# A one-core transformer layer: two one-tile pieces at the opening, an identity made on the chip, and a last addition in two halves

## The chip, the cores and the metric

The kernel runs on one core of one Trainium2 chip. The metric is the device time of one execution in microseconds (us); three runs were timed. One further execution was taken by the hardware profiler; all rows of the profile come from that one. PE is the matrix engine (PEld its weight loads), DVE the vector engine, ACT the scalar engine, POOL the GpSimd engine, SP the engine that issues most transfers.

## The reference

One layer over 256 tokens of width 2048, all in float32. Cut to what matters:

```
D_MODEL = 2048; SEQ = 256; DEPTH = 1; IN_COLS = 6152; D_FF = 5632
def rms_norm(x, g):
    x32 = x.astype(jnp.float32)
    y = x32 * lax.rsqrt(jnp.mean(x32 * x32, axis=-1, keepdims=True) + EPS)
    return (y * g.astype(jnp.float32)).astype(x.dtype)
def hybrid_mixer(h, w_in_l, ...):
    proj = h @ w_in_l
    qa, ka, va, fa, qb, kb, vb = jnp.split(proj, splits, axis=-1)
    ...  # forgetting attention on (qa, ka, va, fa), stick-breaking attention on (qb, kb, vb)
    return merged @ w_out_l
def conv_ffn(h, w_up_l, conv_w_l, conv_b_l, w_down_l):
    u = h @ w_up_l
    ...  # causal depthwise convolution of width 3
    gate, val = jnp.split(u, 2, axis=-1)
    return (jax.nn.silu(gate) * val) @ w_down_l
def reference(x, attn_norm, ...):
    for layer in range(DEPTH):
        h = rms_norm(x, attn_norm[layer])
        x = x + hybrid_mixer(h, ...)
        h = rms_norm(x, ffn_norm[layer])
        x = x + conv_ffn(h, ...)
    return x
```

## The kernel before

Every product is made of three matmuls in the type float32r. A float32 operand is split into a high part (a cast to float32r) and a low part (the operand less its high part), and high by high, low by high and high by low are summed in PSUM. For a weight tile `w_raw`, `split` casts `w_hi` on ACT and then subtracts `w_lo` on DVE. For the tokens, `split_tokens` makes the high part on ACT and the low part on DVE, both scaled by the norm's gain `ga`. The kernel's time is a long row of such products; the tile framework adds the waits, and the order on PE, DVE, ACT and SP is the order in which the code is written out by a list of steps. A step has loads, a preparation (splits) and matmuls. Its loads are issued 6 steps ahead, and its preparation is made 2 steps ahead. Raw weight tiles have 5 buffers, so the load of a sixth waits until a subtraction has freed the first.

The change touches both ends of the program.

**The opening** (`opening`) multiplies the normalised tokens by the first 688 columns of the value weights. The 16 tiles of 128 rows of `w_in` are taken in 8 pieces of two tiles. For each piece the tokens (`xa`, natural layout, 256 tokens on two lots of 128 partitions) are transposed on PE against the identity matrix `ident`, four transposes into one bank `ps_x` (`transposed`), split into `hT` (`split_tokens`), the weights are split, and 24 matmuls of 344 columns follow (`in_three`, twice: two halves of the 688 columns, two lots of tokens, so four banks `acc_v`). The splits of pieces 0 and 1 stand ahead of all matmuls; those of piece i + 2 are written right behind the matmuls of piece i, so that ACT and DVE work on them while PE does piece i + 1. After every second piece, ACT also sums the squares of four tiles of tokens (`squares`). `ident` is the first 128 columns of a table of constants, `cs`, which is loaded from the input `cst`. The gain vector comes as 16 rows (`prow`), is transposed on PE (`columns`, `pp`) and copied to `ga`. All these transfers are issued by SP: tokens 0 and 1, identity, gain rows, tokens 2 and 3, weights 0, and so on.

**The end** is the last product of the down-projection of the feed-forward part. `added` adds a bank of 128 x 512 results to the residual `xb` on DVE, and where that was the last addition of a block, SP stores the block to the output. The last block of all is the second lot of tokens, columns 1024 to 1535.

Of the kernel before, what the change touches and what calls it, by code (L numbers as in the profile page):

```python
# [7 lines left out]

F32 = mybir.dt.float32
F32R = mybir.dt.float32r  # L10
# [4 lines left out]
P = 128  # L15
# [28 lines left out]
def hybrid_layer(  # L44
# [18 lines left out]
):  # L63
    nc = tc.nc
    act, dve = nc.scalar, nc.vector
    act.preload_act_table_set("natural_log_exp_and_others")

    xf = x.rearrange("b s d -> (b s) d")
    of = out.rearrange("b s d -> (b s) d")
# [20 lines left out]


    NC2 = 2 * NFT
    cs = const.tile([P, C_MF], F32, name="cs")
    prow = const.tile([50, P], F32, name="prow")
# [19 lines left out]
    def load_x(k, n, queue=nc.sync):  # L114
        queue.dma_start(x2[:, :, k * P : (k + n) * P], xp[:, :, k * P : (k + n) * P])

    ident = cs[:, C_ID : C_ID + P]
    tri = cs[:, C_TRI : C_TRI + P]
    tri_one = cs[:, C_TRI : C_TRI + 2 * P]
    ones = cs[:, C_ONE : C_ONE + P]  # L120
# [48 lines left out]
    def transposed(k):  # L169
        ps = psb.tile([P, 2, S], F32, name="ps_x", tag="t")  # L170
        for j in range(2):
            for t in range(NT):
                nc.tensor.transpose(  # L173
                    ps[:, j, t * P : (t + 1) * P], x2[:, t, (k + j) * P : (k + j + 1) * P], ident
                )
        return ps

    def split_tokens(ps, k, g):
        for j in range(2):
            i = k + j  # L180
            act.activation(hT[:, i, 0, :], ps[:, j, :], AF.Identity, scale=g[:, i : i + 1])
            dve.scalar_tensor_tensor(
                hT[:, i, 1, :], ps[:, j, :], g[:, i : i + 1], f32(hT[:, i, 0, :]),
                op0=ALU.mult, op1=ALU.subtract,
            )

    def squares(ss, c):
        for t in range(NT):
            act.activation(
                junk, x2[:, t, c * 512 : (c + 1) * 512], AF.Square, accum_out=ss[:, t, c : c + 1]  # L190
            )
# [13 lines left out]
    def new_step(load, sums, prepare, matmuls, follow=None):  # L205
        steps.append((load, sums, prepare, matmuls, follow))
# [31 lines left out]
    def split(raw, a, b):  # L238
        hi = whi.tile([P, 2048], F32R, name="w_hi", tag="w_hi")
        lo = wlo.tile([P, 2048], F32R, name="w_lo", tag="w_lo")  # L240
        n = a * b
        act.copy(hi[:, :n], raw[:, :n])  # L242
        dve.tensor_tensor(lo[:, :n], raw[:, :n], f32(hi[:, :n]), op=ALU.subtract)  # L243
        return (
            hi[:, :n].rearrange("p (a b) -> p a b", a=a),
            lo[:, :n].rearrange("p (a b) -> p a b", a=a),
        )

    def rows_of(w, k0, n, c0, cols):
        return w[k0 * P : (k0 + n) * P, c0 : c0 + cols].rearrange("(k p) c -> p k c", p=P)  # L250

    def in_three(accs, parts, n, lhs, starts, stops, cut=None, middle=None):

        hi, lo = parts
        order = [(i, l, hi) for i in range(n) for l in range(2)] + [(i, 0, lo) for i in range(n)]
        for j, (i, l, r) in enumerate(order):
            if middle and 2 * j == len(order):
                middle()
            for t, o in enumerate(accs):
                nc.tensor.matmul(  # L260
                    o, lhs(i, l, t), r[:, i, :] if cut is None else r[:, i, cut], start=starts and j == 0,
                    stop=stops and j == 3 * n - 1, skip_group_check=len(accs) == 1 and not starts,
                )
# [53 lines left out]
    def opening():  # L317

        banks = []
        x_loads = {0: [(4, 2)], 1: [(6, 2)], 2: [(8, 4)], 3: [(12, 4)]}  # L320
        mem = {}

        def piece(i):
            def loads():
                if i == 0:
                    load_x(0, 2)
                    nc.sync.dma_start(cs[:, :P], cst[:, :P])
                    nc.sync.dma_start(prow[:KT, :], attn_norm[0].rearrange("(n p) -> n p", p=P))
                    load_x(2, 2)
                mem["raw", i] = load(rows_of(wi, 2 * i, 2, V0, 2 * VC))  # L330
                for k, n in x_loads.get(i, ()):
                    load_x(k, n)
                if i == 6:
                    load_parameters()

            def tokens():
                ps = transposed(2 * i)
                if i == 0:
                    columns(ga, prow[:KT, :], KT)
                split_tokens(ps, 2 * i, ga)  # L340
                mem["parts", i] = split(mem["raw", i], 2, 2 * VC)
                if i % 2:
                    squares(ss1, i // 2)
                if i == 7:
                    ready.add("x")

            def matmuls():
                if i == 0:
                    banks.extend([bank_tile(f"acc_v{t}", 2 * j + t) for t in range(NT)] for j in range(2))
                for j in range(2):  # L350
                    in_three(
                        [banks[j][t][:, :VC] for t in range(NT)], mem["parts", i], 2, of_tokens(2 * i),
                        i == 0, i == 7, cut=slice(j * VC, (j + 1) * VC),
                    )
                if i + 2 < 8:
                    tokens_of[i + 2]()

            tokens_of.append(tokens)

            def follow():  # L360
                v = tile_of["v"] = at.tile([P, NT, WF], F32, name="vA", tag="v")
                for j in range(2):
                    for t in range(NT):
                        act.activation(
                            v[:, t, j * VC : (j + 1) * VC], banks[j][t][:, :VC], AF.Identity,
                            scale=rstd1[:, t : t + 1],
                        )
                    yield

            new_step(loads, None, tokens if i < 2 else None, matmuls, follow if i == 7 else None)  # L370

        tokens_of = []
        for i in range(8):
            piece(i)

    opening()


    def last_values():
# [703 lines left out]
    adds = {}  # L1083

    def added(c, ps, t, op=ALU.add):
        xs = x2[:, t, c : c + 512]
        dve.tensor_tensor(xs, xs, ps, op=op)  # L1087
# [146 lines left out]
    def begin(task):  # L1234
        next(task)
        after.append(task)

    hooks[5] = lambda: following.append(factors1())
    hooks[7] = head_parameters
    hooks[13] = lambda: begin(token_sums())  # L1240
# [82 lines left out]
```

## Time and profile before

| what | us |
|---|---|
| median of three runs (1112.0 to 1112.3) | 1112.3 |
| the profiled execution, device time | 1111.69 |
| the profiled execution, span of the trace | 1109.8 |
| PE busy in that span | 1095.4 |
| first matmul of the opening starts at | 10.56 |
| last addition on DVE starts at | 1105.55 |

The span reaches from the first to the last instruction that the profiler saw; 1.9 us of the device time lie around it. All times in rows are from the span's start. PE's busy time has the modelled ends of pipelined matmuls in it, so the pace of a stage is read from the starts of its matmuls.

### The profile page before, as it was taken

To read this page: it belongs to the slowest core of one execution; us is meant where nothing else is said; L and a number is where in the kernel's file an instruction comes from. 1 tells how busy PE (TensorE), PEld (TensorE's weight loads), DVE (VectorE), ACT (ScalarE), POOL (GpSimd) and SP (SyncE) were. 2 spreads that over 40 slices of the span, in tenths; PEclk is the share of its full clock that TensorE was granted. 3 is DMA by queue.
4 is the path that set the end of the run, shared out by engine and by line. 5 is a ranking of instruction groups with operands and counts; after the bars stand their busy time and mean duration, and the time that the engine had idled before them with its cause. 6 is when DMAs were issued, how large, how long until landed. Compare 5 with 4: busy or idle time off the path is not lost.

```text
span 1109.8 us, 14481 instructions
## 1 busy us (share of the span) xinstructions
PE 1095.4 (99%) x5706; PEld 944.7 (85%) x5706; DVE 902.6 (81%) x860; ACT 740.4 (67%) x921; POOL 54.6 (5%) x48
## 2 busy tenths in 40 slices
PE   7999999999999999999999999999999999999998
PEld 6988888888888888888888888888888888888886
DVE  4676888877897577669988898889888888979996
ACT  5645877667676567666767767667776758666853
POOL 0000000000100000000000010000000000000000
PEclk9999999999999999999999999999999999999999
DMA  8757778769778456555979698996969789896994
GB/s 286 273 195 215 235 193 255 174 206 264 246 175 282 132 175 211 190 190 155 301 204 299 214 245 254 247 297 169 292 218 255 265 217 291 214 316 170 299 250 138
DMA packets 174204, 255.41 MB, mean 230 GB/s; under 512 B 4392, under 2 KB 98234, under 8 KB 174138
## 3 DMA queue, kind: packets, MB, share of 16 engines
q1 hardware_dynamic: 152442, 210.47, 56.1%
q0 software_dynamic: 21696, 44.04, 22.4%
q8 instruction: 44, 0.72, 0.3%
q14 instruction: 22, 0.18, 0.0%
HBM read 252.40 MB, written 2.10 MB: 229 GB/s over the span
## 4 chain that ended last, share of the span: by engine, by line
PE 92%; DVE 4%; ACT 1%; issue 1%; DMA 1%; SPq 0%; DVEq 0%; ACTq 0%
PE pu L1069 43%; PE bank_a L260 16%; PE bank_b L260 9%; PE acc_o L260 5%; PE bank_c L260 5%; PE acc_v L260 4%; PE bank_p L260 4%; PE acc L260 2%; PE bank_e L260 2%; DVE w_lo L243 2%; ACT w_hi L242 1%; DMA w_raw<-in_w_in_dram 1%; PE ps_x L173 1%; PE ps_h L605 0%; PE ps_s L686 0%
## 5 line engine op out<-in xcount | busy, mean ns | idle before, releaser
L243 DVE TENSOR_TENSOR w_lo<-w_raw,w_hi 128x2048 fp32r<-128x2048 f32 (+1 forms) x245 | 551.4, 2254 | 156.4 <-ACT w_hi L242 155.8
L242 ACT CAST w_hi<-w_raw 128x2048 fp32r<-128x2048 f32 (+1 forms) x245 | 460.5, 1881 | 229.9 <-PE pu L1069 94.0
L1069 PE MATMUL pu<-hT,w_hi 128*128 128x512 f32 x1408 | 334.8, 390 | 0.7 <-ACT w_hi L242 0.7
L1069 PEld LDWEIGHTS pu<-hT,w_hi 128*128 128x128 f32 x1408 | 262.7, 188 | 54.4 <-ACT w_hi L242 1.2
L1069 PEld LDWEIGHTS pu<-hT,w_lo 128*128 128x128 f32 x1408 | 180.7, 192 | 6.9
L1069 PE MATMUL pu<-hT,w_lo 128*128 128x256 f32 x1408 | 182.9, 283 | 0.0
L999 ACT ACTIVATE tap<-up,ccol 128x256 f32<-128x256 f32 x176 | 74.6, 495 | 0.0
L1115 POOL DMA_DIRECT2D w_raw<-in_w_down_dram x30 | 38.5, 1284 | 722.3 <-DVE w_raw L1133 273.7
L260 PE MATMUL bank_a<-w_hi,hT 128*128 128x512 f32 x160 | 40.7, 396 | 0.0
L260 PE MATMUL bank_b<-w_hi,s 128*128 128x512 f32 x160 | 40.1, 393 | 0.3 <-DVE xb L1087 0.3
L260 PE MATMUL bank_a<-w_hi,g 128*128 128x512 f32 x160 | 40.0, 392 | 0.0
L260 PE MATMUL bank_a<-w_hi,s 128*128 128x512 f32 x160 | 40.0, 392 | 0.0
L260 PE MATMUL acc_v<-w_hi,hT 128*128 128x344 f32 x192 | 35.4, 332 | 3.2 <-ACT w_hi L242 3.2
L260 PEld LDWEIGHTS acc_v<-w_hi,hT 128*128 128x128 f32 x192 | 31.7, 196 | 3.6 <-ACT w_hi L242 3.6
L260 PEld LDWEIGHTS bank_a<-w_hi,hT 128*128 128x128 f32 x160 | 29.2, 189 | 5.6
L260 PEld LDWEIGHTS bank_b<-w_hi,s 128*128 128x128 f32 x160 | 28.9, 189 | 5.7 <-issue 0.5
L260 PEld LDWEIGHTS bank_a<-w_hi,g 128*128 128x128 f32 x160 | 28.9, 189 | 5.2
L260 PEld LDWEIGHTS bank_a<-w_hi,s 128*128 128x128 f32 x160 | 28.9, 189 | 5.2
L992 ACT ACTIVATE gate<-up,ccol 128x256 f32<-128x256 f32 x44 | 24.1, 594 | 12.8 <-DVE s L1045 7.4
L1004 DVE TENSOR_TENSOR gate<-gate,tap 128x512 f32<-128x512 f32 x44 | 30.3, 688 | 2.5 <-ACT tap L999 0.2
L1004 DVE TENSOR_TENSOR val<-val,tap 128x512 f32<-128x512 f32 x44 | 30.3, 689 | 2.3
L985 DVE TENSOR_TENSOR up<-t,R 128x512 f32<-128x512 f32 x44 | 30.5, 692 | 1.5
(273 smaller groups left out, 1404.4 us busy)
## 6 DMA issues: line engine op xcount, KB each, us to landing
w_raw<-in_w_up_dram SPq DMA_DIRECT2D x88, 1024.0 KB, 6.2
w_raw<-in_w_down_dram SPq DMA_DIRECT2D x44, 1024.0 KB, 6.3
w_raw<-in_w_in_dram SPq DMA_DIRECT2D x40, 1024.0 KB, 5.5
w_raw<-in_w_down_dram POOLq DMA_DIRECT2D x30, 1024.0 KB, 10.1
w_raw<-in_w_out_dram SPq DMA_DIRECT2D x16, 1024.0 KB, 7.4
w_raw<-in_w_in_dram SPq DMA_DIRECT2D x12, 688.0 KB, 8.1
w_raw<-in_w_in_dram POOLq DMA_DIRECT2D x8, 1024.0 KB, 9.6
xb<-in_x_dram POOLq DMA_DIRECT2D x4, 512.0 KB, 8.8
```

What stands on the lines that cost most here:

```text
L173: nc.tensor.transpose(ps[:, j, t * P : (t + 1) * P], x2[:, t, (k + j) * P : (k + j + 1) * P], ident)
L242: act.copy(hi[:, :n], raw[:, :n])
L243: dve.tensor_tensor(lo[:, :n], raw[:, :n], f32(hi[:, :n]), op=ALU.subtract)
L260: nc.tensor.matmul(o, lhs(i, l, t), r[:, i, :] if cut is None else r[:, i, cut], start=starts and j == 0, stop=stops and j == 3 * n - 1, s ...
L985: dve.tensor_tensor(u[:, :, 2:], t2, R, op=ALU.mult)
L992: act.activation(a[:, j, :], u[:, j, 2:], AF.Identity, scale=ccol[:, 2, f : f + 1], bias=ccol[:, 3, f : f + 1],)
L999: act.activation(taps[w][:, j, :], u[:, j, w : w + S], AF.Copy, scale=ccol[:, w, f : f + 1])
L1004: dve.tensor_tensor(a, a, tap, op=ALU.add)
L1069: nc.tensor.matmul(acc[:, j, S:] if low else acc[:, j, :], (lo if low else hi)[:, i, j * P : (j + 1) * P], hT[:, k, 0, :] if low else hT[: ...
L1115: nc.gpsimd.dma_start(mem[weights].rearrange("p (a b) -> p a b", a=4), plus, accum_op=ALU.add)
```

## The change

The opening has nine pieces: two of one tile, then seven of two tiles. For the two small pieces, both transposed by the first four transposes, a loop of their own issues 12 matmuls each: high weights by high tokens into all four banks, high weights by low tokens, low weights by high tokens. In the first of them the high part of the weights is cast by DVE in place of ACT (`cast` with `dve.tensor_copy`), between the copy of `ga` and the first low part of tokens. The gain rows are transposed ahead of the tokens.

The order of the transfers is: tokens 0 and 1, the two small weight pieces, tokens 2 and 3, weights of the third piece, and so on, all on SP. The gain rows go to ACT's queue, ahead of ACT's load of its function table. The identity is no longer loaded: `make_identity` fills it on POOL with a memset and an affine select. The hooks that were set at steps 5, 7 and 13 are counted from the opening's new length.

At the end, the one last addition is made in two halves of 256 columns, the first stored by SP, the second by ACT.

```
+    prow = const.tile([50, P], F32, name="prow")
+    act.dma_start(prow[:KT, :], attn_norm[0].rearrange("(n p) -> n p", p=P))
+    act.preload_act_table_set("natural_log_exp_and_others")
...
     ident = cs[:, C_ID : C_ID + P]
+    make_identity(nc, ident)
...
+    def cast(raw, n, copy):
         hi = whi.tile([P, 2048], F32R, name="w_hi", tag="w_hi")
         lo = wlo.tile([P, 2048], F32R, name="w_lo", tag="w_lo")
+        copy(hi[:, :n], raw[:, :n])
+        return hi, lo
+    def split(raw, a, b):
+        return subtracted(raw, *cast(raw, a * b, act.copy), a, b)
...
-        x_loads = {0: [(4, 2)], 1: [(6, 2)], 2: [(8, 4)], 3: [(12, 4)]}
+        sizes = [1, 1] + [2] * 7
+        x_loads = {0: (0, 2), 1: (2, 2), 2: (4, 2), 3: (6, 2), 4: (8, 4), 5: (12, 4)}
...
                 if i == 0:
-                    load_x(0, 2)
-                    nc.sync.dma_start(cs[:, :P], cst[:, :P])
-                    nc.sync.dma_start(prow[:KT, :], attn_norm[0].rearrange("(n p) -> n p", p=P))
-                    load_x(2, 2)
-                mem["raw", i] = load(rows_of(wi, 2 * i, 2, V0, 2 * VC))
+                    load_x(*x_loads[i])
+                mem["raw", i] = load(rows_of(wi, k0, n, V0, 2 * VC))
+                if 0 < i < 6:
+                    load_x(*x_loads[i])
...
+                if n == 1 and i == 0:
                     columns(ga, prow[:KT, :], KT)
+                    ps = mem["ps"] = transposed(0)
+                    hi, lo = cast(mem["raw", 0], 2 * VC, dve.tensor_copy)
+                    split_tokens(ps, 0, ga, 1)
+                    mem["parts", 0] = subtracted(mem["raw", 0], hi, lo, 1, 2 * VC)
+                elif n == 1:
+                    split_tokens(mem["ps"], 0, ga, 1, 1)
+                    mem["parts", 1] = split(mem["raw", 1], 1, 2 * VC)
...
+                if n == 1:
+                    hi, lo = mem["parts", i]
+                    for l, w in ((0, hi), (1, hi), (0, lo)):
+                        for j in range(2):
+                            for t in range(NT):
+                                nc.tensor.matmul(
+                                    banks[j][t][:, :VC], of_half(hT[:, k0], l, t),
+                                    w[:, 0, j * VC : (j + 1) * VC], start=i == l == 0 and w is hi, stop=False,
+                                )
...
     def added(c, ps, t, op=ALU.add):
-        xs = x2[:, t, c : c + 512]
-        dve.tensor_tensor(xs, xs, ps, op=op)
         adds[t, c] = adds.get((t, c), 0) + 1
-        if adds[t, c] == (1 if t and c % 1024 == 0 else 2) * (len(FFN_PARTS) - 1) + 1:
-            nc.sync.dma_start(of[t * P : (t + 1) * P, c : c + 512], xs)
+        done = adds[t, c] == (1 if t and c % 1024 == 0 else 2) * (len(FFN_PARTS) - 1) + 1
+        last_one = done and (t, c) == (NT - 1, 1024)
+        for queue, h, n in ((nc.sync, 0, 256), (act, 256, 256)) if last_one else ((nc.sync, 0, 512),):
+            xs = x2[:, t, c + h : c + h + n]
+            dve.tensor_tensor(xs, xs, ps[:, h : h + n], op=op)
+            if done:
+                queue.dma_start(of[t * P : (t + 1) * P, c + h : c + h + n], xs)
```

What stands at the head of POOL's row of instructions with the change (line numbers of the changed file, of the function that makes the identity where masks.py is named). In the built program the instruction called ISA in row 7 has the name PseudoReloadLibraryIndex, library 0.

```order
3 L1340 MEMSET const-bfloat16-1.0 128x1
4 L1340 MEMSET const-uint8-127 128x1
5 L1350 UNCONDITIONAL_BRANCH
6 masks.py:197 MEMSET cs 128x128
7 masks.py:199 ISA
8 masks.py:199 AFFINE_SELECT cs<-cs 128x128
9 L518 DMA w_raw<-in_w_in_dram 128x4x512 x8
```

Rows 6 to 8 are new; before, the transfers of row 9 followed the branch directly.

DVE at the start of the opening before: the copy of the gains, the two low parts of the tokens, then the low part of the weights of piece 0, and so on.

```order
1 L167 COPY ga<-pp 128x16
2 L182 SCALAR_TENSOR_TENSOR hT<-ps_x,ga,hT 128x256 x2
3 L243 TENSOR_TENSOR w_lo<-w_raw,w_hi 128x1376
4 L182 SCALAR_TENSOR_TENSOR hT<-ps_x,ga,hT 128x256 x2
5 L243 TENSOR_TENSOR w_lo<-w_raw,w_hi 128x1376
```

DVE at the same place with the change:

```order
1 L170 COPY ga<-pp 128x16
2 L244 CAST w_hi<-w_raw 128x688
3 L185 SCALAR_TENSOR_TENSOR hT<-ps_x,ga,hT 128x256
4 L252 TENSOR_TENSOR w_lo<-w_raw,w_hi 128x688
5 L185 SCALAR_TENSOR_TENSOR hT<-ps_x,ga,hT 128x256
6 L252 TENSOR_TENSOR w_lo<-w_raw,w_hi 128x688
7 L185 SCALAR_TENSOR_TENSOR hT<-ps_x,ga,hT 128x256 x2
8 L252 TENSOR_TENSOR w_lo<-w_raw,w_hi 128x1376
```

The cast of the first weights stands on DVE ahead of every low part, and the tokens of tiles 2 and 3 (row 7) come behind both small pieces.

More of the change, by code (lines that the diff above doesn't have):

```diff
@@ L7 @@
 from concourse._compat import with_exitstack
+from concourse.masks import make_identity
 F32 = mybir.dt.float32
@@ L92, in hybrid_layer @@
     NC2 = 2 * NFT
+    prow = const.tile([50, P], F32, name="prow")
+    act.dma_start(prow[:KT, :], attn_norm[0].rearrange("(n p) -> n p", p=P))
+    act.preload_act_table_set("natural_log_exp_and_others")
     cs = const.tile([P, C_MF], F32, name="cs")
-    prow = const.tile([50, P], F32, name="prow")
     bf = const.tile([P, NH], F32, name="bf")
@@ L176, in transposed, with split_tokens @@
         return ps
-    def split_tokens(ps, k, g):
-        for j in range(2):
+    def split_tokens(ps, k, g, n=2, j0=0):
+        for j in range(j0, j0 + n):
             i = k + j
@@ L319, in opening @@
         banks = []
-        x_loads = {0: [(4, 2)], 1: [(6, 2)], 2: [(8, 4)], 3: [(12, 4)]}
+        sizes = [1, 1] + [2] * 7
+        starts = [sum(sizes[:i]) for i in range(len(sizes))]
+        last = len(sizes) - 1
+        x_loads = {0: (0, 2), 1: (2, 2), 2: (4, 2), 3: (6, 2), 4: (8, 4), 5: (12, 4)}
         mem = {}
         def piece(i):
+            k0, n = starts[i], sizes[i]
             def loads():
                 if i == 0:
-                    load_x(0, 2)
-                    nc.sync.dma_start(cs[:, :P], cst[:, :P])
-                    nc.sync.dma_start(prow[:KT, :], attn_norm[0].rearrange("(n p) -> n p", p=P))
-                    load_x(2, 2)
-                mem["raw", i] = load(rows_of(wi, 2 * i, 2, V0, 2 * VC))
-                for k, n in x_loads.get(i, ()):
-                    load_x(k, n)
-                if i == 6:
+                    load_x(*x_loads[i])
+                mem["raw", i] = load(rows_of(wi, k0, n, V0, 2 * VC))
+                if 0 < i < 6:
+                    load_x(*x_loads[i])
+                if i == 7:
                     load_parameters()
             def tokens():
-                ps = transposed(2 * i)
-                if i == 0:
+                if n == 1 and i == 0:
                     columns(ga, prow[:KT, :], KT)
[L340 to L344, printed above, removed]
+                    ps = mem["ps"] = transposed(0)
[5 more added lines that the diff above has]
+                    mem["parts", 1] = split(mem["raw", 1], 1, 2 * VC)
+                else:
+                    split_tokens(transposed(k0), k0, ga)
+                    mem["parts", i] = split(mem["raw", i], 2, 2 * VC)
+                if k0 % 4 == 2:
+                    squares(ss1, k0 // 4)
+                if i == last:
                     ready.add("x")
@@ L349, in matmuls @@
                     banks.extend([bank_tile(f"acc_v{t}", 2 * j + t) for t in range(NT)] for j in range(2))
[L350 to L355, printed above, removed]
+                if n == 1:
[7 more added lines that the diff above has]
+                                )
+                else:
+                    for j in range(2):
+                        in_three(
+                            [banks[j][t][:, :VC] for t in range(NT)], mem["parts", i], 2, of_tokens(k0),
+                            False, i == last, cut=slice(j * VC, (j + 1) * VC),
+                        )
+                if i + 2 <= last:
                     tokens_of[i + 2]()
@@ L368, in follow @@
                     yield
-            new_step(loads, None, tokens if i < 2 else None, matmuls, follow if i == 7 else None)
+            new_step(loads, None, tokens if i < 2 else None, matmuls, follow if i == last else None)
         tokens_of = []
-        for i in range(8):
+        for i in range(len(sizes)):
             piece(i)
     opening()
+    V_END = len(steps)
     def last_values():
@@ L1236, in begin @@
         after.append(task)
-    hooks[5] = lambda: following.append(factors1())
-    hooks[7] = head_parameters
-    hooks[13] = lambda: begin(token_sums())
+    hooks[V_END - 3] = lambda: following.append(factors1())
+    hooks[V_END - 1] = head_parameters
+    hooks[V_END + 5] = lambda: begin(token_sums())
     hooks[D_UNIT + 7] = reload_x
```

4 lines of the change are left out of this document (1 added, 3 removed).

## The prediction

> **What bounds the kernel now.** I read the page first, then busy time in three stretches, then the chain of waits of the opening.
>
> ```profile
> PE 1095.4 (99%) x5706; PEld 944.7 (85%) x5706; DVE 902.6 (81%) x860; ACT 740.4 (67%) x921; POOL 54.6 (5%) x48
> ```
>
> ```profile
> core 0: us, PE busy (x) PEld busy (x) DVE busy (x) ACT busy (x) POOL busy (x), PEclk, DMA share, GB/s
> 0.00:10.56 10.56, 2.42 (x10) 1.61 (x10) 1.16 (x4) 3.62 (x5) 0.20 (x4) 1.00 0.72 239
> 10.56:1105.52 1094.96, 1092.97 (x5697) 943.07 (x5697) 900.70 (x856) 736.82 (x917) 54.39 (x44) 1.00 0.79 231
> 1105.52:1109.80 4.28, 0.00 (x0) 0.00 (x0) 0.69 (x1) 0.00 (x0) 0.00 (x0) 1.00 0.16 61
> ```
>
> PE is idle for 14.4 us: about 8 before the first product at 10.56, 4.3 behind the last, and 2 (1094.96 - 1092.97) in all the rest. A product that starts earlier or later at the front therefore moves the whole program one for one, and nothing in the middle is there to swallow it. The chain says what the front waits for:
>
> ```profile
> 2.67 6.48 DMA w_raw<-in_w_in_dram
> 9.14 0.02 issue
> 9.17 1.35 ACT w_hi L242
> 10.56 5.83 PE acc_v L260 x24
> ```
>
> The weights of piece 0 (688 KB) are issued at 2.67, land at 9.15, and are cast until 10.5. The identity isn't on that chain, as the timeline shows:
>
> ```profile
> 0.74 0.43 SPq L115 DMA_DIRECT2D xa<-in_x_dram  x1
> 1.23 0.46 SPq L327 DMA_DIRECT2D cs<-in_cst_dram  x1
> 1.73 0.42 SPq L328 DMA_DIRECT2D prow<-in_attn_norm_dram  x1
> 4.18 0.72 PEld L173 LDWEIGHTS ps_x<-cs,xa 128*128 128x128 f32 x4 [4.18 <-DMA xa<-in_x_dram]
> 4.21 1.09 PE L173 MATMUL ps_x<-cs,xa 128*128 128x128 f32 x4 [4.21 <-DMA cs<-in_cst_dram]
> 5.76 0.47 ACT L181 ACTIVATE hT<-ps_x,ga 128x256 fp32r<-128x256 f32 x1 [3.74 <-DVE ga L167]
> ```
>
> With identity and tokens there at 4.21, the first high tokens are ready at 6.23, 2.02 later. That is 4.3 us ahead of the weights: slack that the loaded identity has and the made one may use up.
>
> **Term 1: the weights.** Ahead of the first weights SP no longer issues identity, gain rows and tokens 2 and 3; they are issued at 1.23 in place of 2.67, and are 344 KB. Tokens of 256 KB landed by 4.18; by 9.15 another 1016 KB (64 + 8 + 256 + 688) had. At that pace 344 KB take 1.7 us: landed at 5.9. The transfer of the tokens, 3.44 us after its issue, gives the other end, 1.23 + 3.44 = 4.7. I take 5.3. The cast on DVE is bounded by two rows:
>
> ```profile
> L1224 DVE CAST masksR<-masks 128x512 fp32r<-128x512 f32 x1 | 0.4, 420 | 0.0
> L1223 DVE CAST identR<-cs 128x128 fp32r<-128x128 f32 x1 | 0.2, 216 | 0.0
> ```
>
> 204 ns for 384 columns more, so 688 take 0.51. High weights: 5.8. Behind that cast, a new wait of DVE for a transfer, stand the first low tokens (0.48) and low weights; PE asks for them four and eight matmuls after the first product, so it costs nothing.
>
> **Term 2: the identity.** POOL starts with the others, at 0.74. The memset and the select have no row of their size; I take 0.2 each, DVE's cast of 128 x 128 (POOL's own memsets of one column take 0.1). Between them stands an instruction that reloads POOL's library, for which no row exists. Below it could cost nothing. Nearest in kind is ACT's table load, 1.28; nearest in place are transfers of the opening, which take 3.44 (tokens), 6.48 (first weights), or, for 8 KB behind a full queue, 8.0; nearest by engine are POOL's own loads, 10.1 from issue to landing:
>
> ```profile
> 0.73 1.28 ACT L66 ACT_TABLE_LOAD   x1 [0.73 <-PEq L1308]
> xa<-in_x_dram SPq DMA_DIRECT2D x4, 256.0 KB, 7.5
> prow<-in_ffn_norm_dram SPq DMA_DIRECT2D x1, 8.0 KB, 8.0
> w_raw<-in_w_down_dram POOLq DMA_DIRECT2D x30, 1024.0 KB, 10.1
> DMA  0006858899979999999999999999999999637503
> ```
>
> (The last row is the transfer engines' busy share from 0 to 26 us, in tenths, 0.65 us a digit: from 2 us on they are busy, from 5 on nearly full.) A library is code in memory, wanted at 0.95 by the engine, just as SP's queue fills. So I take 7.0, between 6.48 and 7.5, both of transfers of that moment, and keep 0 and 10.1 as ends. Identity at 0.74 + 0.2 + 7.0 + 0.2 = 8.15; high tokens 2.02 later, 10.2. The gains' transpose stands ahead of the tokens' now, but the same members are in the 2.02.
>
> The Trainium skill, GPSIMD Engine Reference, § 2.1 Instruction dispatch, says that the first call to a freshly loaded kernel pays an instruction load of about 6 us with no instruction of its own in the profile. By that figure the identity would come at 7.15 and the sum below would be 1.0 lower, 1112.1; no run here shows it yet.
>
> **Term 3: the pace of the first pieces.** The first product starts at the later of 5.8 and 10.2: 10.2, against 10.56 before. What follows is read from these rows:
>
> ```profile
> 14.16 1.59 PE L260 MATMUL acc_v<-w_hi,hT 128*128 128x344 f32 x8
> 16.22 0.60 PE L173 MATMUL ps_x<-cs,xa 128*128 128x128 f32 x4
> 16.58 1.50 PE L260 MATMUL acc_v<-w_hi,hT 128*128 128x344 f32 x8
> 17.89 0.48 ACT L181 ACTIVATE hT<-ps_x,ga 128x256 fp32r<-128x256 f32 x1 [0.55 <-DVE hT L182]
> 18.26 1.33 ACT L242 CAST w_hi<-w_raw 128x1376 fp32r<-128x1376 f32 x1
> 18.54 1.43 PE L260 MATMUL acc_v<-w_hi,hT 128*128 128x344 f32 x8
> 19.62 1.59 DVE L243 TENSOR_TENSOR w_lo<-w_raw,w_hi 128x1376 fp32r<-128x1376 f32 x1 [0.74 <-ACT w_hi L242]
> 20.45 0.60 PE L173 MATMUL ps_x<-cs,xa 128*128 128x128 f32 x4
> 20.80 0.40 PE L260 MATMUL acc_v<-w_hi,hT 128*128 128x344 f32 x1
> ```
>
> The first 12 matmuls took 14.16 - 10.56 = 3.60 (slow pace), 12 later ones 20.45 - 18.54 = 1.91, four transposes 0.36 (16.22 to 16.58), a whole piece 4.22 (16.58 to 20.80). From the transposes of a piece to the end of its cast pass 19.59 - 16.22 = 3.37, and that chain now stands behind a piece of half the size. With the change: piece 0 from 10.2 to 13.8; transposes of tiles 2 and 3; piece 1 to 16.1; transposes of 4 and 5 to 16.4. The cast for tiles 2 and 3 is ready at 13.8 + 3.4 = 17.2, so PE waits 0.75. The low weights come 1.6 later, at 18.8, while eight matmuls last to 18.5: 0.3 more. The piece ends at 21.4, the next begins at 21.75, where it began at 20.80 before. On ACT its weights stand behind the squares of four tiles:
>
> ```profile
> 14.16 0.63 ACT L189 ACTIVATE junk<-xa 128x512 f32<-128x512 f32 x1
> 15.45 0.19 ACT L189 ACTIVATION_READ_ACCUMULATOR junk<-xa 128x1 f32 x1
> ```
>
> They take 14.16 to 15.64, about 1.5: from 17.2 to 18.7, then the tokens of 4 and 5 wait for DVE, and the cast is done at about 21.5, in time. From there the pieces run 4.22 apart as before. The opening costs 21.75 - 20.80 = +0.95.
>
> Hidden: SP's shorter list; the half subtractions (0.8 each, half of 1.59) under the slow first matmuls, which would cost up to 0.8 if PE ran at the later pace at once; the load of the gain rows ahead of ACT's table load, which delays ACT by an issue of 0.4 at 0.7 with nothing due on ACT before 5; the sixth weight load, which waits for the first low weights, at 11.6, as it did before, and whose cast is due only at 25 (21.75 and a piece, less the cast's lead).
>
> **Term 4: the end.**
>
> ```profile
> L1087 DVE TENSOR_TENSOR xb<-xb,bank_a 128x512 f32<-128x512 f32 x3 | 2.1, 685 | 1.5 <-PE bank_a L260 1.4
> DMA to landing us min/median/max: 2.2/3.6/7.2
> SPq L1318 <- DMA out_dram<-xb: 1.8, 1, 1.8
> ```
>
> The addition (685 ns) is followed by a store of 256 KB that lands 2.2 after its issue, and SP waits 1.8 for it before it may end. ACT waits for the second half with nothing behind it in its queue. Two halves end about 0.15 later on DVE (a second instruction's fixed part), the second store is half as long; 256 KB at the opening's 205 KB/us (1016 KB in 4.97) are 1.25, so half of it is up to 0.6 saved. Bounds: +0.2 (nothing saved) and -0.5; I take -0.2.
>
> By the Trainium skill, DMA: Bandwidth & Descriptors, § Rules for kernel authors, stores from several queues run on the same 16 engines and save issue time alone. By that rule the end would give about 0, and the sum 1113.3.
>
> **Sum.** +0.95 - 0.2 = +0.75. The profiled execution would go from 1111.69 to 1112.4; its 1111.69 lies 0.6 under the median of the runs, 1112.3, which goes to 1113.1. 0.2% is 2.2 us, about what a measurement of this kernel can tell from no change.
>
> **Rivals.**
> A, the forecast: a reload of 6 to 8.5 us, so 1112.1 - 0.5 to 1114.6 + 0.5 with 0.5 for the pace, thus 1111.6 to 1115.1. Chance 0.50.
> B, the reload is cheap: under about 2.5 us nothing waits for it, the tokens at 4.2 and the weights at 5.8 do. First product at 5.85; the start that I compare (20.80 before; 11.55 behind the first product with the change) falls to 17.4, so -3.4, with the end -3.6: 1108.7, give or take 0.8. For it: POOL's other instructions here are short, and 1.28 for ACT's table. Against it: ACT's load began on an empty queue. Chance 0.27.
> C, the identity becomes the bound: the reload is drawn out by the loads beside it, as POOL's own transfers are (10.1). Identity at 11.25, first product at 13.3, +4.05 - 0.2 = +3.85: 1116.2. It decides from a reload of about 8.5, where the sum passes +2.2. For it: the transfer engines are nearly full from 5 us on, and 8 KB took 8.0. Chance 0.20.
> D, the pieces stall otherwise: half pieces give ACT and DVE half the time, and if the chain of 3.37 stays behind PE for several pieces, 0.5 to 1.5 more on top of A: up to 1115. Chance 0.03.
>
> Faster: B but for its edge, 0.25. Slower: C, 0.07 of A's upper edge, and half of D: 0.28. Within: the rest, 0.47. The range from 1108.4 to 1116.2 leaves out a third of B and half of C, under 0.2; A alone is 1111.6 to 1115.1.
>
> **What would show it.** Right: ps_x waiting for POOL at the front and starting near 8.5, the first acc_v near 10.2 behind ACT's hT and not behind weights, a gap on PE of under 1 us ahead of the third piece, a piece start near 21.75. B: ps_x near 4.2, waiting for xa. C: ps_x at 10 or later. Wrong altogether: a gap on PE in the middle that wasn't there, or a first product waiting for w_raw.

## The result and the profile after

The changed kernel takes 1109.39 us in the median of 8 runs (1108.66 to 1111.64), the kernel before 1112.30 in 8 runs beside them; the ratio is 0.9975, with a 95% interval of 0.9964 to 0.9986. It is faster by 2.9 us, where 1113.1, slower by 0.8, was forecast. This is what rival B said, the cheap reload (1108.7, give or take 0.8, chance 0.27); the forecast's range of 1108.4 to 1116.2 takes in 1109.4 by that rival alone.

The timeline of the changed kernel, POOL's first rows and then PE, DVE and ACT up to the first product (start, duration, what; in brackets the idle time before and what ended it):

```profile
0.74 0.20 POOL masks.py:197 MEMSET cs<- 128x128 f32 x1 [0.29 <-POOLq L1340]
1.02 0.29 POOL masks.py:199 TENSOR_SCALAR_AFFINE_SELECT cs<-cs 128x128 f32<-128x128 f32 x1
...
3.53 0.26 PE L169 MATMUL pp<-cs,prow 16*128 16x16 f32 x1 [3.53 <-DMA prow<-in_attn_norm_dram]
...
4.40 1.11 PE L176 MATMUL ps_x<-cs,xa 128*128 128x128 f32 x4 [0.61 <-DMA xa<-in_x_dram]
...
5.26 0.52 DVE L244 CAST w_hi<-w_raw 128x688 fp32r<-128x688 f32 x1 [1.26 <-DMA w_raw<-in_w_in_dram]
5.55 0.47 ACT L184 ACTIVATE hT<-ps_x,ga 128x256 fp32r<-128x256 f32 x1 [3.04 <-PE ps_x L176]
...
6.08 2.66 PE L373 MATMUL acc_v<-w_hi,hT 128*128 128x344 f32 x8 [0.56 <-ACT hT L184]
```

The library reload stands between the first two rows. The memset ends at 0.94 and the select starts at 1.02, so the reload has 0.08 us at most. The identity is there at 1.31, and nothing waits for POOL: the gains' transpose waits for the gains, the tokens' transposes for the tokens, the cast for the weights. The first product starts at 6.08, where it started at 10.56.

The chain of waits at the front, ahead of the first product, was the weights' transfer and ACT's cast. In this execution it is now the first tokens:

```profile
0.74 3.61 DMA xa<-in_x_dram
4.40 1.13 PE ps_x L176 x4
5.55 0.48 ACT hT L184
6.08 3.81 PE acc_v L373 x12
9.88 0.87 PE ps_x L176 x4
```

Tokens and weights are nearly level there: DVE's cast of the weights ends at 5.78, 0.3 ahead of the first product, and in two other profiles of the same order of transfers (e1 and e8 below) the first product waits for that cast instead, at 5.89 and 5.97.

The 4.48 won there are not all kept. The timeline between the first piece and the compared start (20.80 before):

```profile
9.68 1.05 PE L176 MATMUL ps_x<-cs,xa 128*128 128x128 f32 x4
10.39 1.74 PE L373 MATMUL acc_v<-w_hi,hT 128*128 128x344 f32 x8
...
12.59 0.60 PE L176 MATMUL ps_x<-cs,xa 128*128 128x128 f32 x4
...
13.56 1.53 PE L269 MATMUL acc_v<-w_hi,hT 128*128 128x344 f32 x8 [0.37 <-ACT w_hi L244]
...
15.19 0.62 PEld L269 LDWEIGHTS acc_v<-w_lo,hT 128*128 128x128 f32 x4 [0.38 <-DVE w_lo L252]
...
17.81 0.60 PE L176 MATMUL ps_x<-cs,xa 128*128 128x128 f32 x4
...
18.16 1.51 PE L269 MATMUL acc_v<-w_hi,hT 128*128 128x344 f32 x8
```

At the third piece PE waits for ACT's cast and then, shown on its weight loads (PEld), for DVE's low weights, as the forecast had it. The compared start is 18.16, 2.64 earlier than before; with 0.2 at the end that is the 2.9 of the medians.

The end, in the timeline after (two rows) and then in that of before (one row):

```profile
1104.86 0.75 DVE L1120 TENSOR_TENSOR xb<-xb,bank_a 128x256 f32<-128x256 f32 x2 [1.95 <-PE bank_a L269]
1105.64 0.38 ACTq L1122 DMA_DIRECT2D out_dram<-xb  x1
```

```profile
1105.55 0.69 DVE L1087 TENSOR_TENSOR xb<-xb,bank_a 128x512 f32<-128x512 f32 x1 [1.43 <-PE bank_a L260]
```

From the start of the last addition to the end of the span (1108.9) pass 4.04, before 4.25 (1105.55 to 1109.8).

The profiled execution of the changed kernel was the slowest of its 8, 1111.64. Its last addition is only 0.7 earlier than before, because PE loses time again behind the opening. Busy time from the first product to the last addition shows it (the stretch, its length, then the busy time of PE and of the other engines), after and then with the library experiment below (e8), which has the same opening for PE and the same end and kept its lead of 2.7:

```profile
6.08:1104.80 1098.72, 1095.24 (x5701) 942.80 (x5701) 901.75 (x859) 738.09 (x919) 54.43 (x44) 1.00 0.80 231
```

```profile
5.97:1102.80 1096.83, 1094.78 (x5701) 943.70 (x5701) 901.76 (x859) 737.94 (x919) 54.41 (x44) 1.00 0.79 232
```

PE's idle time there is 3.5 in the one and 2.05 in the other (2.0 before). The trace also shows where the lead went. At 1057.33 the changed kernel is still level with e8 (1057.23, the same matmuls); its loss lies behind that, where from 1020 on ACT's casts wait 17.8 in all for the weights of the down-projection (13.9 in e8, 8.2 before) and the chain of waits runs over their transfers, while in e8 it runs over PE alone. Since e1 and e8 kept their lead, that loss belongs to the one execution and not to the change. Why those weights landed later in it stays open.

### The profile page after: what moved, and what is told of

It reads as the page before. It is cut to its first block, busy times and chain, and to the rows that moved or that the text cites. A ratio compares the mean times of both kernels' runs of the same rounds, so it can differ in the third digit from the quotient of the medians.

```text
span 1108.9 us, 14494 instructions
## 1 busy us (share of the span) xinstructions
PE 1096.6 (99%) x5706; PEld 943.7 (85%) x5706; DVE 903.2 (81%) x863; ACT 739.9 (67%) x921; POOL 55.1 (5%) x50
## 4 chain that ended last, share of the span: by engine, by line
PE 83%; DVE 8%; DMA 4%; issue 3%; ACT 2%; DVEq 0%; ACTq 0%; POOLq 0%
PE pu L1098 39%; PE bank_a L269 14%; PE bank_b L269 8%; PE acc_o L269 5%; PE bank_c L269 4%; DMA w_raw<-in_w_down_dram 4%; PE bank_p L269 4%; DVE w_lo L252 4%; PE acc_v L269 4%; PE bank_e L269 2%; ACT w_hi L244 1%; PE ps_x L176 1%; PE ps_h L634 0%; DVE xb L1120 0%; DVE w_raw L1165 0%
## 5 line engine op out<-in xcount | busy, mean ns | idle before, releaser
L252 DVE TENSOR_TENSOR w_lo<-w_raw,w_hi 128x2048 fp32r<-128x2048 f32 (+2 forms) x246 | 551.7, 2245 | 156.2 <-ACT w_hi L244 155.0
L244 ACT CAST w_hi<-w_raw 128x2048 fp32r<-128x2048 f32 (+2 forms) x245 | 459.9, 1878 | 229.9 <-PE pu L1098 89.0
L269 PE MATMUL acc_v<-w_hi,hT 128*128 128x344 f32 x176 | 31.2, 323 | 0.4 <-ACT w_hi L244 0.4
L269 PE MATMUL acc_o<-w_hi,oSb 128*128 128x512 f32 x128 | 31.3, 396 | 0.0
## 6 DMA issues: line engine op xcount, KB each, us to landing
w_raw<-in_w_down_dram POOLq DMA_DIRECT2D x30, 1024.0 KB, 10.2
```

Source lines behind the costliest of these rows:

```text
L269: nc.tensor.matmul(o, lhs(i, l, t), r[:, i, :] if cut is None else r[:, i, cut], start=starts and j == 0, stop=stops and j == 3 * n - 1, s ...
```

## The experiments

The spread from execution to execution is 1 us and more, so each run is read by its median and also by two landmarks of its profile, the first product and the compared start. The first tokens land anywhere between 3.7 and 4.4 in these profiles, and PE's change from its slow pace to the later one comes now earlier, now later. Both move the landmarks of like kernels: by up to 0.4 among the changed kernel, e1, e4 and e8, and by 0.5 between the kernel before and e2, whose openings are the same (e2's first product is 0.17 earlier, its compared start 0.49 later). A difference of less than about 0.5 at the compared start can't be told from this spread.

| kernel | first product | compared start | last addition to end | median us |
|---|---|---|---|---|
| before | 10.56 | 20.80 | 4.25 | 1112.1 to 1112.5 |
| changed | 6.08 | 18.16 | 4.04 | 1109.4 |
| e1, whole last addition | 5.89 | 17.74 | 4.27 | 1109.1 |
| e2, before with the halves | 10.39 | 21.29 | 4.04 | 1111.95 |
| e3, identity loaded | 6.67 | 18.56 | 4.00 | 1109.5 |
| e4, fills that were moved | 6.08 | 18.16 | 4.06 | 1109.4 |
| e4b, identity made late | 11.54 | 23.66 | 4.83 | 1114.75 |
| e5, two-tile pieces | 7.95 | 18.73 | 4.12 | 1109.7 |
| e6, tokens first | 7.51 | 19.59 | 4.06 | 1110.4 |
| e8, another library | 5.97 | 18.02 | 4.01 | 1109.1 |
| e9, cast first | 5.81 | 16.98 | 4.07 | 1108.7 |
| e11, PE at work early | 5.95 | 15.96 | 4.06 | 1106.8 |
| e12, both | 6.27 | 17.47 | 4.02 | 1108.2 |

**The end alone.** e1 is the changed kernel with the last addition whole:

```
-        for queue, h, n in (...) if last_one else ((nc.sync, 0, 512),):
+        for queue, h, n in (...) if False else ((nc.sync, 0, 512),):
```

> The changed kernel with the last addition and its store whole again. If the gain is made in the opening, the third weight load's piece starts at 18.16 as with the whole change, the stretch from the last addition's start to the end is 4.25 again in place of 4.0, and the time is 1109.6, 0.2 above the changed kernel's 1109.4. If the gain is made at the end, the time goes back to about 1112.

e2 is the kernel before with only the new `added`:

```
+        for queue, h, n in ((nc.sync, 0, 256), (act, 256, 256)) if last_one else ((nc.sync, 0, 512),):
+            xs = x2[:, t, c + h : c + h + n]
+            dve.tensor_tensor(xs, xs, ps[:, h : h + n], op=op)
+            if done:
+                queue.dma_start(of[t * P : (t + 1) * P, c + h : c + h + n], xs)
```

> The kernel before with nothing but the halves of the last addition. If the gain is made in the opening: that piece's start stays at 20.80, the end is 0.2 shorter, the time 1112.1. If it is made at the end: about 1109.5. If a store on a second queue costs a wait of its own: up to 1112.5.

e1: 1109.11, ratio to before 0.9974 (0.9964 to 0.9985). e2: 1111.95, ratio 0.9998 (0.9989 to 1.0007). The gain is in the opening. The last stretch is 4.25 and 4.27 with a whole addition and 4.00 to 4.12 in nearly all kernels with halves, so the halves are worth 0.2, less than the totals can tell. (The one exception is e4b's 4.83: there SP waits 2.6 for the last stores to land, where it waits 1.8 before, with the change and in e1, e6 and e8. Why is open.)

**Is the made identity what pays?** e3 loads it again:

```
-    make_identity(nc, ident)
...
                     load_x(*x_loads[i])
+                    nc.sync.dma_start(cs[:, :P], cst[:, :P])
                 mem["raw", i] = load(rows_of(wi, k0, n, V0, 2 * VC))
```

> The changed kernel with the identity loaded again, issued by SP behind the first tokens, in place of the one made on POOL. If the order of the transfers and the small pieces carry the gain, the weights come one issue (0.47) and some 0.2 of transfer later, the first product starts near 6.5 (6.08 with the change), the compared start is near 18.6, the time near 1109.9. If the made identity carries it, the first product goes back toward 8 or later and the time to 1111 to 1112.

1109.51, ratio 0.9977 (0.9967 to 0.9986). In its timeline the identity, there at 4.19, holds up the gains' transpose alone; the first product waits for DVE's cast, and so for the weights:

```profile
4.19 0.25 PE L168 MATMUL pp<-cs,prow 16*128 16x16 f32 x1 [4.19 <-DMA cs<-in_cst_dram]
...
6.01 0.52 DVE L243 CAST w_hi<-w_raw 128x688 fp32r<-128x688 f32 x1 [1.35 <-DMA w_raw<-in_w_in_dram]
```

The cast starts 0.75 later than with the change (5.26), behind one more issue on SP and 64 KB. At the compared start that is 0.4 to 0.8 (18.56 against 17.7 to 18.2), hardly more than like kernels differ by. Most of the gain doesn't need the made identity.

**A late identity.** The forecast said what an identity at 8 us would do. e4 writes 14 fills of a scratch tile ahead of it on POOL:

```
+NDELAY = 14
...
+    for _ in range(NDELAY):
+        nc.gpsimd.memset(junk, 0.0)
     make_identity(nc, ident)
```

> The changed kernel with 14 fills of a 128 x 512 scratch tile on POOL ahead of the identity, some 0.5 each (an estimate from 0.20 for 128 x 128 and 0.10 for 128 x 1), so that the identity is made 7 us later. By the forecast's own reckoning for an identity at 8.2 to 8.4: first product near 10.2, compared start 21.75, so +3.6 on the changed kernel, 1113.0. If the opening has slack that the forecast missed, the compared start is below 20.8 and the time under 1112. If what a late start costs is carried on in full, the start is 12.1 behind the first product, 22.3, and the time 1113.5.

1109.36; it says nothing about a late identity. POOL's order is not the written one: the identity's memset stands behind one fill and its select behind two, and the other twelve come after:

```profile
1.20 0.21 POOL masks.py:197 MEMSET cs<- 128x128 f32 x1
...
1.91 0.28 POOL masks.py:199 TENSOR_SCALAR_AFFINE_SELECT cs<-cs 128x128 f32<-128x128 f32 x1
2.14 7.17 POOL L122 MEMSET junk<- 128x512 f32 x12
```

e4b fills the table in which the identity lies, so the identity has to come behind all 17 fills:

```
+NDELAY = 17
...
+    for _ in range(NDELAY):
+        nc.gpsimd.memset(cs, 0.0)
     make_identity(nc, ident)
```

> The changed kernel with 17 fills of the 398 columns of the constant table on POOL ahead of the identity, which lies in that table, so that nothing can be moved in front of them: some 0.45 each (0.52 was measured for 512 columns), so the identity comes some 7.5 later, near 8.9. By the forecast's own reckoning for a late identity: first product near 10.7, compared start about 22, time 1113.0 to 1113.5. If the opening makes up for a late start (slack that the forecast missed), the compared start is under 20.8 and the time under 1112.

1114.75, ratio 1.0023 (1.0013 to 1.0032), slower than before. Its timeline:

```profile
9.31 0.29 POOL masks.py:199 TENSOR_SCALAR_AFFINE_SELECT cs<-cs 128x128 f32<-128x128 f32 x1
9.65 0.28 PE L172 MATMUL pp<-cs,prow 16*128 16x16 f32 x1 [9.65 <-POOL cs masks.py:199]
...
11.54 2.66 PE L376 MATMUL acc_v<-w_hi,hT 128*128 128x344 f32 x8 [0.56 <-ACT hT L187]
...
15.15 1.05 PE L179 MATMUL ps_x<-cs,xa 128*128 128x128 f32 x4
15.86 1.80 PE L376 MATMUL acc_v<-w_hi,hT 128*128 128x344 f32 x8
...
23.66 1.50 PE L272 MATMUL acc_v<-w_hi,hT 128*128 128x344 f32 x8
```

The first product comes 1.94 behind the identity, the compared start 12.12 behind the first product (12.08 with the change), and the total rises by 5.4 where the start moved 5.5. Nothing in the opening makes up for a late identity. Here it is complete at 9.60; at the forecast's 8.15 the time would be about 1113.3 (an estimate: 1114.75 less the 1.45 between the two). So had the reload cost what the forecast took, the forecast's sign would have been right.

**Does a reload cost where another library is named?** The changed kernel's reload names library 0, which might have been there already. e8 puts an instruction ahead whose reload, in the built program, names library 1:

```
+    nc.gpsimd.memset(R2[:1, :P], 0.0)
+    nc.gpsimd.partition_broadcast(ident, R2[:1, :P])
     make_identity(nc, ident)
```

> The changed kernel with a broadcast over the partitions on POOL ahead of the identity, written to the same columns; it is an instruction of another library of POOL, so that a reload is in front of it that is not of the library there from the start. If a reload is cheap whichever library is named: identity under 2.5, first product near 6.1, time 1109.4. If a reload costs only where the library is not there already: POOL stands still for 6 to 10 ahead of the broadcast, first product near 10 to 13, compared start 21.7 to 25, time 1113 to 1116. The forecast's 7.0 would give an identity near 8.8 and a start near 22.

```profile
0.74 0.19 POOL L120 MEMSET R<- 1x128 f32 x1 [0.29 <-POOLq L1342]
1.09 0.42 POOL L121 PARTITION_BROADCAST cs<-R  x1 [0.16 <-POOL R L120]
1.57 0.21 POOL masks.py:197 MEMSET cs<- 128x128 f32 x1
1.86 0.29 POOL masks.py:199 TENSOR_SCALAR_AFFINE_SELECT cs<-cs 128x128 f32<-128x128 f32 x1
```

1109.11, ratio 0.9972 (0.9962 to 0.9982). The reload of library 1 lies in the 0.16 behind the first memset. In the built program of e8 it is the only reload: none stands ahead of the select, and yet the select starts 0.08 behind the end of its memset (1.78 to 1.86), as in the changed kernel, where library 0's reload stands between the two. So that reload adds nothing that can be seen. Nor do the DMA queues show a library on its way; these are the queue rows of instructions (packets, MB, share), the same in e3, which makes no identity and has no reload, and in e8:

```profile
q8 instruction: 44, 0.72, 0.3%
q14 instruction: 22, 0.18, 0.0%
```

(Some other runs have one packet of 0.02 MB more, with a reload, as e5, or without one, as e2.) So in a profiled execution a reload costs under 0.2, whichever of the two libraries it names, and the medians leave no room for one of several us: e4b shows what a late identity does to them. Whether a library is brought in once, when the program is loaded, no run here shows.

**Size against order.** e5 keeps the order, the made identity and the end, and goes back to eight two-tile pieces:

```
-        sizes = [1, 1] + [2] * 7
-        x_loads = {0: (0, 2), 1: (2, 2), 2: (4, 2), 3: (6, 2), 4: (8, 4), 5: (12, 4)}
+        sizes = [2] * 8
+        x_loads = {0: (0, 2), 1: (4, 2), 2: (6, 2), 3: (8, 4), 4: (12, 4)}
...
                 mem["raw", i] = load(rows_of(wi, k0, n, V0, 2 * VC))
+                if i == 0:
+                    load_x(2, 2)
...
```

> The changed kernel with eight two-tile pieces, as before, but with the new order and queues of the transfers, the made identity and the halves at the end. If the order carries the gain: weights (688 KB right behind the first tokens) land near 7.2, the cast on ACT takes 1.34, first product 8.6, compared start 10.24 behind it as before, 18.8; time 1110.0. If the small pieces carry it: first product at 9.8 or later, start above 20, time 1111.3 or more.

e6 keeps the small pieces and puts tokens 2 and 3 ahead of the first weights again:

```
                     load_x(*x_loads[i])
+                    load_x(2, 2)
                 mem["raw", i] = load(rows_of(wi, k0, n, V0, 2 * VC))
-                if 0 < i < 6:
+                if 1 < i < 6:
```

> The changed kernel with the tokens of tiles 2 and 3 issued ahead of the first weights, as before. If the order of these 256 KB counts: first weights land 1.2 later (256 KB at 205 KB/us), near 6.5, first product 7.0 in place of 6.08, compared start 18.9 to 19.1, time 1110.2. If only the size of the first weights counts: first product within 0.3 of 6.1 and time 1109.5.

e5: 1109.73, ratio 0.9976 (0.9967 to 0.9985). e6: 1110.44, ratio 0.9983 (0.9974 to 0.9992). The timeline of e5, whose cast on ACT follows the tokens with no wait, and then the one row of e6 that counts:

```profile
6.57 1.33 ACT L244 CAST w_hi<-w_raw 128x1376 fp32r<-128x1376 f32 x1
...
7.95 2.66 PE L269 MATMUL acc_v<-w_hi,hT 128*128 128x344 f32 x8
...
18.73 1.50 PE L269 MATMUL acc_v<-w_hi,hT 128*128 128x344 f32 x8
```

```profile
6.84 0.52 DVE L244 CAST w_hi<-w_raw 128x688 fp32r<-128x688 f32 x1 [3.04 <-DMA w_raw<-in_w_in_dram]
```

With two-tile pieces the compared start is already 2.07 earlier than before. The small pieces win 1.9 at the first product (7.95 to 6.08) but only 0.6 to 1.0 at the compared start, since the third piece then waits. The order of the 256 KB of tokens is worth 1.58 at the cast (6.84 against 5.26) and 1.4 to 1.9 at the compared start. So the order carries the larger part of the gain, and half or more of what the small pieces win is given back two pieces later. The medians have the same order, 1109.11 in e8, which ran beside these two, then e5 and e6, but their intervals overlap; the split rests on the landmarks. The move of the gain rows to ACT's queue was not run by itself.

**What is left in the opening.** e9 casts the third piece's weights ahead of its tokens on ACT:

```
+                    if i == 2:
+                        hi, lo = cast(mem["raw", i], 2 * 2 * VC, act.copy)
+                        split_tokens(ps, k0, ga)
+                        mem["parts", i] = subtracted(mem["raw", i], hi, lo, 2, 2 * VC)
```

> The changed kernel with the high cast of the third piece's weights on ACT ahead of that piece's tokens. ACT is idle from 7.7 to 10.8 there. If the two gaps of PE at the third piece (0.37 and 0.38) come from the cast's place behind the tokens, both go: compared start 17.4 in place of 18.16, time 1108.7. If the weights of that piece land too late (issued at 2.7, the cast waits beyond 10), the tokens come later and the gaps stay or grow: start 18.2 to 18.7, time 1109.4 to 1110.

e11 gives PE work from the identity on, ahead of anything that is needed:

```
+NWARM = 12
...
+    wt = psb.tile([P, 512], F32, name="warm", tag="t")
+    for _ in range(NWARM):
+        nc.tensor.transpose(wt[:, :P], ident, ident)
```

> The changed kernel with 12 transposes of the identity on PE, to a bank that nobody reads, ahead of the gains' transpose, from 1.3 on. In every run the first 12 matmuls of 344 columns go at 0.33 apart and later ones at 0.16, and the pace changes some 6 us behind PE's first work (4.4 to 10.4 with the change, 9.7 to 15.9 with the late identity). If the pace follows how long PE has worked, it changes by about 7.5 now, the first piece lasts 2.0 to 3.0 in place of 3.6, but the third piece's weights and tokens then come late, and the compared start is 16.8 to 17.8; time 1108.0 to 1109.0. If the pace hangs on something else (the transfers, the time from the start), the first product stays at 6.1, the start at 18.1 and the time at 1109.4.

e12 has both edits:

> Both edits together: the transposes of the identity ahead, and the third piece's cast ahead of its tokens. If each takes away what it should: compared start 15.5 to 16.8, time 1106.8 to 1108.1. If the third piece's weights are the bound by then: no better than the better of the two alone.

e9: 1108.67, ratio 0.9967 (0.9954 to 0.9980). e11: 1106.81, ratio 0.9955 (0.9940 to 0.9970), the fastest of all (four of its five runs lie at 1106.6 to 1107.1, one at 1108.9). e12: 1108.16, ratio 0.9962 (0.9948 to 0.9976). The timeline of e11:

```profile
1.36 2.82 PE L124 MATMUL warm<-cs 128*128 128x128 f32 x12 [1.36 <-POOL cs masks.py:199]
...
5.95 1.50 PE L377 MATMUL acc_v<-w_hi,hT 128*128 128x344 f32 x8 [0.68 <-DVE w_hi L248]
...
7.92 0.60 PE L180 MATMUL ps_x<-cs,xa 128*128 128x128 f32 x4
...
11.34 1.52 PE L273 MATMUL acc_v<-w_hi,hT 128*128 128x344 f32 x8
...
15.96 1.50 PE L273 MATMUL acc_v<-w_hi,hT 128*128 128x344 f32 x8
```

The first piece lasts 1.97 (5.95 to 7.92) in place of 3.60, from its first matmul on. The compared start is 2.2 earlier than with the change, 0.8 better than the best that was expected. The edit uses the early identity; with the loaded one, there at 4.19 in e3, these transposes could not have begun before.

In e9 the compared start is 16.98, 1.18 earlier than with the change. Its timeline:

```profile
12.04 0.60 PE L176 MATMUL ps_x<-cs,xa 128*128 128x128 f32 x4
...
12.39 1.50 PE L269 MATMUL acc_v<-w_hi,hT 128*128 128x344 f32 x8
...
13.97 0.62 PEld L269 LDWEIGHTS acc_v<-w_lo,hT 128*128 128x128 f32 x4 [0.36 <-DVE w_lo L252]
```

The third piece follows its transposes with no gap (0.35), which is 0.6 of it. The second gap, for DVE's low weights, is still there (0.36). Another 0.27 is a first product at 5.81, and 0.24 a second piece that was at the later pace sooner; both lie within what like kernels differ by, so they need not come from the edit. In e9 the third piece's weights only land at 9.2, and once PE is at its later pace from the start that is too late to cast first. The timeline of e12:

```profile
9.66 1.35 ACT L248 CAST w_hi<-w_raw 128x1376 fp32r<-128x1376 f32 x1 [1.98 <-DMA w_raw<-in_w_in_dram]
...
14.47 0.90 PE L273 MATMUL acc_v<-w_lo,hT 128*128 128x344 f32 x4 [0.92 <-DVE w_lo L256]
```

ACT stands still for 1.98 with the tokens behind it, and PE then waits 0.92 for the low weights. Together the two edits are worse than the second alone: the rival of e12's expectation (no better than the better one), and worse than it said.

## Why the prediction was wrong

**Term 2, the identity: the step that failed.** The reload was taken as 7.0, between 0 and 10.1; it is 0.08 at most here and 0.16 with another library, so the identity is there at 1.31 and not at 8.15, and the first product starts at 6.08 behind tokens and weights and not at 10.2 behind the identity. The rest of the term held: memset 0.20 (forecast 0.2), select 0.29 (0.2), identity to first product 1.94 in e4b (2.02). The price was taken from transfers of that moment, on the argument that a library is code in memory that is wanted just then. No row showed such a transfer; the rows nearest by engine were POOL's memsets at 0.1, and the low end of the range, 0, was the true one. The Trainium skill, GPSIMD Engine Reference, § 2.1 Instruction dispatch, has about 6 us for the first call to a freshly loaded kernel; the trace doesn't show it in this case, neither for the select (0.29, its start 0.08 behind the memset) nor for the broadcast (0.42, its start 0.16 behind).

**Term 1, the weights: right.** Landed at 5.3 by the forecast, cast started at 5.26. Cast 0.51 by the forecast, 0.52 measured. The 256 KB of tokens cost 1.58 in e6, a little more than 205 KB/us would give (1.25).

**Term 3, the pace: right in kind, 0.5 short.** From first product to compared start 11.55 were reckoned, 12.08 measured here and 12.12 in e4b. The first piece is exact (3.60). The four transposes behind it still go at the slow pace, 0.71 for 0.36 (9.68 to 10.39), and the second piece lasts 2.20 for 1.94 (10.39 to 12.59). The first gap is 0.61 for 0.75 (13.56 less 12.59 and 0.36), and the third piece with its second gap lasts 4.25 (13.56 to 17.81), where 4.2 was reckoned. What was too short is the slow pace: the sum ended it with the first 12 matmuls, as in the kernel before, but it ends at no fixed place. The first eight products of the second piece, in e1 and then in e8, whose openings are alike:

```profile
10.04 1.51 PE L373 MATMUL acc_v<-w_hi,hT 128*128 128x344 f32 x8
```

```profile
10.25 2.37 PE L375 MATMUL acc_v<-w_hi,hT 128*128 128x344 f32 x8
```

With the change they took 1.74, and in e1 the start came 11.85 behind the first product (5.89 to 17.74), so part of the 0.5 is this one profile.

**Term 4, the end: right.** -0.2 forecast, 4.25 to 4.04 measured. By the rule of the Trainium skill, DMA: Bandwidth & Descriptors, § Rules for kernel authors, that transfers from several queues save issue time alone, it would have been about 0 (an estimate); that rule is not refuted, since the runs don't tell the shorter last store from the second queue.

**The rivals.** That the time lies in the stated range is owed to rival B, not to the mechanism that was forecast. B gave a first product at 5.85 (6.08), a compared start at 17.4 (18.16) and 1108.7 (1109.4); its short fall is Term 3's 0.5 and the later first product. What spoke against it, that ACT's table load of 1.28 began on an empty queue, was no evidence on POOL. A and C both had the identity as the bound. e4b brings that about by fills, at 1114.75; in this kernel nothing does, since the identity is there at 1.31. D did not come: behind the third piece the pieces start 4.24 and 4.23 apart (18.16, 22.40, 26.63), as before.

## What to carry to other kernels

Where the sign of a forecast hangs on one price without a row, take the nearest row of the same engine, and ask the trace for the traffic that the dearer price would need; the most likely case should not be built on an analogy with transfers. At a start that waits for memory, first ask which bytes stand ahead of the bytes that are waited for: the order of 256 KB was worth more here than halving the first piece. And read a landmark some pieces behind the front, since what the front wins is partly given back at the next wait.

## What the runs showed of the hardware that was not expected

A reload of POOL's library took at most 0.08 (library 0, where e8 has the same 0.08 without one) and 0.16 (library 1), with the same packets on the instruction queues as without a reload (44 and 22, in e8 and e3).

PE's slow pace at the start goes with its own work rather than with the time or the transfers. The first eight products of 344 columns took 2.66 when PE began at 3.5 and also when it began at 9.65; after 12 transposes that nobody reads, from 1.36 on, they took 1.50. The granted clock stands at 1.00 in all these stretches and doesn't show it. The Trainium skill, TensorE: Matmul & The Clock Gate, Part 1, says that PE runs at half its clock until it has been busy for about 3.4 us, and that the place of the change varies from run to run. The runs agree in both, though the slow pace stands longer than that here. In e11 the pace is the later one 4.6 behind the first transpose (1.36 to 5.95), with some 4 of it work. With the change the slow pace still stood for the four transposes at 9.68, 6.2 behind the first work and 3.6 behind the first product, from which on PE was busy throughout; and e1 and e8, with like openings, change at different places (the eight products of 1.51 and 2.37 above).

In e4, DVE's cast of 128 x 688 took 0.85 while POOL was filling memory; in the changed kernel it took 0.52, and DVE's other instructions beside those fills were no longer than elsewhere (0.47, 0.86). The row is from the timeline of e4:

```profile
5.09 0.85 DVE L247 CAST w_hi<-w_raw 128x688 fp32r<-128x688 f32 x1 [0.95 <-DMA w_raw<-in_w_in_dram]
```

It is one instruction in one profile, so no more than a hint that POOL's work can slow a cast on DVE.
